# A two-layer decoder trunk on one core: three transposes moved from TensorE to VectorE in 32x32 blocks, x's sums of squares moved to GpSimd

## The chip, the core and the metric

The kernel runs on one core of a Trainium2 chip. A core has five engines that run their own instruction streams and meet through semaphores: TensorE (PE; its weight loads stand apart as PEld), VectorE (DVE), ScalarE (ACT), GpSimd (POOL) and SyncE (SP), which here issues nearly all transfers to the core's 16 DMA engines. Each engine takes its instructions in the order in which the program has them. The metric is the device time of one execution in microseconds, as the median of several runs; lower is better.

## What is computed

Batch 1, 256 positions, width 2048, two layers in float32. Layer 0 is a spatial gate (gMLP) beside cross-attention into 256 memory tokens, layer 1 latent attention (MLA) beside the same cross-attention; each is followed by a gated ConvFFN, and a last norm follows. Cut to what the change touches:

```python
def rmsnorm(x, g):
    return x * lax.rsqrt(jnp.mean(x * x, axis=-1, keepdims=True) + EPS) * g

def spatial_gating(z_u, z_v, g_v, w_sp, b_sp):
    u = gelu(z_u)
    v = rmsnorm(gelu(z_v), g_v)
    w = w_sp * jnp.tril(jnp.ones((CHUNK, CHUNK)))          # 12 heads of 128x128
    sv = einsum('gts,bnsgc->bntgc', w, v_in_chunks) + b_sp
    return u * sv

for l in range(2):
    z = rmsnorm(x, g_mix[l]) @ w_in[l]
    main = spatial_gating(...) if l == 0 else mla_attention(...)
    x = x + concat([main, memory_attention(...)]) @ w_out[l]
    x = x + conv_ffn(rmsnorm(x, g_ffn[l]), ...)
return rmsnorm(x, g_final)
```

## The kernel before

**Layout.** The residual `self.x` is kept in SBUF transposed: 16 blocks of 128 channels on the partitions, 256 positions along the free axis. The input `x` and the memory tokens come from HBM with the positions on the partitions (`xtok`, `mtok`), so they have to be turned. `token_transpose` (L395) does it on PE: four 128x128 transposes by the identity into one PSUM bank, from which `put_x` (L452) or `put_mem` (L446) writes the operand.

**Products.** Every weight chunk (128x1024, 512 KB) is loaded into `raw` (4 buffers), ACT writes a rounded high part `whi` (4 buffers) and DVE the rest `wlo` (5 buffers), with a gain factor where one applies (`chunk`, L98; L118 and L119 with gains and in two halves, L113 and L114 without). The activations are split the same way (`xhl`, `memhl`: high and low halves side by side). A product is the sum of three: high by high, high by low, low by high. `gemm_fm` (L158) holds the weights still and streams 256 positions: 16 matmuls with `whi` (L152, L153), then 8 with `wlo` (L155) for a chunk; `gemm_tm` (L190) streams 512 weight columns: 12 matmuls a chunk (L184, L185 with `wlo`, L186). Small pieces of other work are hung between chunks as hooks, by chunk number.

**The start.** `start` (L430) builds the memory keys and values of both layers, in this order: keys of layer 0 (`first_keys`, L477, its order written by hand), values of layer 0 (`gemm_tm`, 8 chunks, called c0 to c7 here), keys of layer 1 (`gemm_fm`, 8 chunks, called k0 to k7), values of layer 1. In the hooks of the last three the input x is loaded (four transfers of 512 KB), turned (8 calls for two blocks each: four transposes, two L245 on ACT and two L246 on DVE for `xhl` with the gain `g_mix`, and an ACT copy into `self.x`, L455), and its sums of squares are made by ACT from `xtok` (`token_squares`, L406, eight pieces) and reduced by DVE (`token_rstd`, L414). `spread` (L420) turns a per-position factor into a broadcast along the free axis: two diagonal matrices by DVE and two fp32 products. `scale_keys` (L466) multiplies the keys of layer 0 on POOL.

**Spatial weights.** `spatial_load` (L754) brings the 12 heads in one transfer, into the buffer that `memhl` held. `spatial_turn` (L760) transposes four at a time on PE, and DVE multiplies by the causal mask `keep` on the way out of PSUM (L765).

**The end.** In the second ConvFFN x is turned back into `xt` (positions on the partitions) by `turn` (L1110) in the hooks of one gemm: 32 transposes on PE, 8 ACT copies.

**Order.** The Tile scheduler sets the order on every engine by its own simulated timeline, but for the stretches under `manual_schedule`; the hooks only say where in the program a piece stands. In the stretch from c0 to k7 the hand-written order holds for SP alone, and only up to c7.

## Time and profile before

| | us |
|---|---|
| median of 3 runs (2058.31 to 2058.63) | 2058.41 |
| the profiled execution | 2058.79 |
| its span, first to last instruction | 2057.0 |
| PE busy | 2046.9 |
| DVE busy | 1396.0 |
| ACT busy | 1085.6 |
| POOL busy | 142.0 |
| transfers on SP's queue, mean share of the 16 DMA engines | 58.5% of the span |

The busy times are sums over stages with different limits, so only PE's says something by itself: hardly any time is left in which it has nothing to do. A matmul's busy time overlaps the next one's (a 128x256 matmul is shown with some 0.28 us, and the next starts 0.11 us later), so what a matmul costs is read from the distance of starts.

### The profile page before, as it was taken

To read this page: it belongs to the slowest core of one execution; us is meant where nothing else is said; L and a number is where in the kernel's file an instruction comes from. 1 tells how busy PE (TensorE), PEld (TensorE's weight loads), DVE (VectorE), ACT (ScalarE), POOL (GpSimd) and SP (SyncE) were. 2 spreads that over 40 slices of the span, in tenths; PEclk is the share of its full clock that TensorE was granted. 3 is DMA by queue.
4 is the path that set the end of the run, shared out by engine and by line. 5 is a ranking of instruction groups with operands and counts; after the bars stand their busy time and mean duration, and the time that the engine had idled before them with its cause. 6 is when DMAs were issued, how large, how long until landed. Compare 5 with 4: busy or idle time off the path is not lost.

```text
span 2057.0 us, 39914 instructions
## 1 busy us (share of the span) xinstructions
PE 2046.9 (100%) x16348; PEld 1979.9 (96%) x16348; DVE 1396.0 (68%) x2113; ACT 1085.6 (53%) x1588; POOL 142.0 (7%) x200
## 2 busy tenths in 40 slices
PE   9999999999999999999999999999999999999998
PEld 8989999999999999999999999999988999889996
DVE  6656766777656766457788786776765667646765
ACT  7754744555434555345555575455544555435554
POOL 0000013100000000000043241300000000000000
PEclk9999999999999999999999999999999999999999
DMA  8565555566556665566655635565655666556654
GB/s 288 188 217 176 160 193 198 190 195 195 195 195 195 193 193 193 194 193 194 195 195 176 187 118 178 187 204 177 193 193 194 196 195 195 187 193 195 197 181 154
DMA packets 207692, 392.58 MB, mean 191 GB/s; under 512 B 14158, under 2 KB 23188, under 8 KB 207380
## 3 DMA queue, kind: packets, MB, share of 16 engines
q1 hardware_dynamic: 207316, 389.48, 58.5%
q8 instruction: 128, 2.10, 0.4%
q10 hardware_dynamic: 192, 0.54, 0.1%
q14 instruction: 56, 0.46, 0.1%
HBM read 387.88 MB, written 2.10 MB: 190 GB/s over the span
## 4 chain that ended last, share of the span: by engine, by line
PE 99%; ACT 0%; DVE 0%; DMA 0%; issue 0%; ACTq 0%
PE ps L152 26%; PE ps L153 26%; PE ps L155 26%; PE ps L185 6%; PE ps L184 6%; PE ps L186 6%; PE ps L507 1%; PE ps L400 0%; PE ps L583 0%; PE ps L584 0%; PE ps L582 0%; PE ps L1001 0%; PE ps L790 0%; PE ps L1115 0%; PE ps L1029 0%; DMA graw<-in_g_mem 0%
## 5 line engine op out<-in xcount | busy, mean ns | idle before, releaser
L114 DVE TENSOR_TENSOR wlo<-raw,whi 128x1024 fp32r<-128x1024 f32 x660 | 818.4, 1243 | 531.1 <-ACT whi L113 525.0
L113 ACT ACTIVATE whi<-raw 128x1024 fp32r<-128x1024 f32 x660 | 700.6, 1062 | 857.8 <-PE ps L153 632.3
L152 PE MATMUL ps<-xhl,whi 128*128 128x256 f32 x3264 | 763.2, 277 | 0.0
L153 PE MATMUL ps<-xhl,whi 128*128 128x256 f32 x3264 | 761.2, 276 | 0.0
L153 PEld LDWEIGHTS ps<-xhl,whi 128*128 128x128 f32 x3264 | 612.9, 188 | 0.3
L152 PEld LDWEIGHTS ps<-xhl,whi 128*128 128x128 f32 x3264 | 612.7, 188 | 0.3
L155 PE MATMUL ps<-xhl,wlo 128*128 128x256 f32 x3264 | 436.7, 276 | 0.0
L155 PEld LDWEIGHTS ps<-xhl,wlo 128*128 128x128 f32 x3264 | 400.5, 188 | 0.0
L152 PE MATMUL ps<-h,whi 128*128 128x256 f32 x704 | 163.6, 276 | 0.0
L153 PE MATMUL ps<-h,whi 128*128 128x256 f32 x704 | 163.6, 276 | 0.0
L185 PE MATMUL ps<-wlo,h 128*128 128x512 f32 x354 | 137.2, 388 | 0.0
L184 PE MATMUL ps<-whi,h 128*128 128x512 f32 x354 | 136.8, 388 | 0.0
L186 PE MATMUL ps<-whi,h 128*128 128x512 f32 x354 | 136.8, 388 | 0.0
L153 PEld LDWEIGHTS ps<-h,whi 128*128 128x128 f32 x704 | 132.0, 188 | 0.0
L152 PEld LDWEIGHTS ps<-h,whi 128*128 128x128 f32 x704 | 131.8, 188 | 0.0
L152 PE MATMUL ps<-mainhl,whi 128*128 128x256 f32 x512 | 119.6, 277 | 0.0
L153 PE MATMUL ps<-mainhl,whi 128*128 128x256 f32 x512 | 119.3, 276 | 0.0
L694 ACT ACTIVATE c<-a,cT 128x256 f32<-128x256 f32 x176 | 99.4, 588 | 0.0
L153 PEld LDWEIGHTS ps<-mainhl,whi 128*128 128x128 f32 x512 | 96.0, 188 | 0.0
L152 PEld LDWEIGHTS ps<-mainhl,whi 128*128 128x128 f32 x512 | 95.9, 188 | 0.0
L155 PE MATMUL ps<-h,wlo 128*128 128x256 f32 x704 | 94.1, 276 | 0.0
L232 DVE TENSOR_TENSOR a<-ps,rbc 128x256 f32<-128x256 f32 x176 | 70.0, 418 | 27.6 <-PE ps L155 27.6
(321 smaller groups left out, 2258.6 us busy)
## 6 DMA issues: line engine op xcount, KB each, us to landing
raw<-in_w_ffn_up SPq DMA_DIRECT2D x352, 512.0 KB, 3.5
raw<-in_w_ffn_down SPq DMA_DIRECT2D x176, 512.0 KB, 3.9
raw<-in_w_out SPq DMA_DIRECT2D x64, 512.0 KB, 4.2
raw<-in_w_in_a SPq DMA_DIRECT2D x56, 512.0 KB, 4.3
raw<-in_w_mem_kv SPq DMA_DIRECT2D x31, 512.0 KB, 4.9
raw<-in_w_in_b SPq DMA_DIRECT2D x16, 512.0 KB, 4.6
raw<-in_w_kv_a SPq DMA_DIRECT2D x9, 512.0 KB, 3.6
raw<-in_w_uq SPq DMA_DIRECT2D x12, 384.0 KB, 3.8
```

What stands on the lines that cost most here:

```text
L113: nc.scalar.activation(hi[:, :n], raw[:, :n], AF.Copy)
L114: nc.vector.tensor_tensor(lo[:, :n], raw[:, :n], hi[:, :n].bitcast(F32), ALU.subtract)
L152: mm(acc[:, :S], wh, x[:, :S], start=first, stop=False)
L153: mm(acc[:, :S], wh, x[:, S:], start=False, stop=False)
L155: mm(acc[:, :S], wl, x[:, :S], start=False, stop=last)
L184: mm(acc, xh, wh, start=first, stop=False)
L185: mm(acc, xh, wl, start=False, stop=False)
L186: mm(acc, xl, wh, start=False, stop=last)
L232: self.nc.vector.tensor_tensor(out, acc[:, :S], r, ALU.mult)
L507: nc.tensor.matmul(acc[:, :S], w[:, o : o + P], x, start=k == 0 and n == 0, stop=k == NB - 1 and n == 2)
L694: nc.scalar.activation(c, a, AF.Identity, scale=w(2), bias=w(3))
```

## The change

- **x.** `block_load` replaces `token_load` for x: eight transfers of 256 KB with pieces of 32 elements (128 bytes) place x's 32x32 blocks in `xraw`, 32 channels of position blocks to a partition, two transfers for each of four calls. DVE's transpose of 32x32 blocks (`nc.vector.transpose`, 128x256 for one channel block) then writes `self.x`; `split_gain` reads it from SBUF instead of PSUM, and POOL squares and adds (`square_add`, 31 instructions). `x_rstd` makes the broadcast factor `rb` and the per-position factor `rt` from these sums, with one 128x256 product and two of one column. The 32 PE transposes of x, the eight ACT squares, the eight ACT copies and `spread(self.rb, self.rt)` go.
- **Hooks.** The loads of x start two chunks later; the turns stand in other hooks; `scale_keys` stands earlier. `diag` gets a second buffer.
- **Spatial weights.** Four transfers with 128-byte pieces instead of one with 512-byte rows; three DVE transposes 128x512; POOL multiplies by `keep` in place. 12 PE transposes and three DVE multiplications go.
- **The end.** Four DVE transposes 128x1024 into `xs` (2 buffers) and 16 transfers SBUF to SBUF with 128-byte pieces into `xt`, instead of 32 PE transposes and eight ACT copies.

```diff
@@ -392,6 +392,13 @@
         c = slice(k0 * P, k1 * P)
         self.nc.sync.dma_start(out=tok[:, :, c], in_=src.rearrange("(a p) c -> p a c", p=P)[:, :, c])
 
+    def block_load(self, src, raw, q, half):
+        s = src.rearrange("(i m) (k q j) -> q i m k j", m=8, q=4, j=32)
+        m = slice(4 * half, 4 * half + 4)
+        for p in (q, q + 1):
+            o = raw[32 * p : 32 * (p + 1), m].rearrange("i m k j -> i (m k) j")
+            self.nc.sync.dma_start(out=o, in_=s[p, :, m].rearrange("i m k j -> i (m k) j"))
+
     def token_transpose(self, tok, k0, k1, put):
         for k in range(k0, k1, 2):
             acc = self.psum()
@@ -421,7 +428,7 @@
         nc = self.nc
         acc = self.psum()
         for tb in range(2):
-            dg = self.tmp(self.cp, [P, P], "diag", 1)
+            dg = self.tmp(self.cp, [P, P], "diag", 2)
             nc.vector.tensor_scalar(dg, self.ident, r[:, tb : tb + 1], None, ALU.mult)
             nc.tensor.matmul(acc[:, tb * P : (tb + 1) * P], self.ones, dg, start=True, stop=True)
         nc.scalar.activation(out, acc[:, :S], AF.Copy)
@@ -436,10 +443,11 @@
         self.mv = [pool.tile([P, 2, MW], F32, name=self.uid("mv")) for pool in (self.mk, self.cp)]
         self.rt = self.cp.tile([P, 2], F32, name="rt0")
         self.rb = self.tmp(self.cp, [P, S], "rbc", 2)
+        self.ssum = self.tmp(self.cp, [P, S], "ssum", 2)
         with tc.tile_pool(name="st", bufs=1) as st:
             self.gp = st
             mtok = st.tile([P, 2, D], F32, name="mtok")
-            xtok = st.tile([P, 2, D], F32, name="xtok")
+            xraw = st.tile([P, 8, NB, 32], F32, name="xraw")
             mrt = st.tile([P, 2], F32, name="mrt")
             mrb = st.tile([P, S], F32, name="mrb")
 
@@ -449,19 +457,25 @@
                 nc.scalar.activation(hi, a, AF.Copy)
                 nc.vector.tensor_tensor(mhl[:, k : k + 2, S:], a, hi.bitcast(F32), ALU.subtract)
 
-            def put_x(k, acc):
-                for i in range(2):
-                    self.split_gain(self.xhl[k + i], acc[:, i * S : (i + 1) * S], self.gain("g_mix", k + i))
-                nc.scalar.activation(self.x[:, k : k + 2, :], acc.rearrange("p (k s) -> p k s", k=2), AF.Copy)
+            def xturn(k0, k1):
+                for k in range(k0, k1):
+                    nc.vector.transpose(out=self.x[:, k, :].rearrange("p (i m) -> p m i", m=8), in_=xraw[:, :, k, :])
+                    self.split_gain(self.xhl[k], self.x[:, k, :], self.gain("g_mix", k))
+                    self.square_add(self.ssum, self.x[:, k, :], k == 0, self.cp)
+
+            def x_rstd():
+                self.rstd_bc(self.rb, self.ssum, D)
+                acc = self.psum()
+                for tb in range(2):
+                    nc.tensor.matmul(acc[:, tb : tb + 1], self.ssum[:, tb * P : (tb + 1) * P], self.ones[:, :1], start=True, stop=True)
+                self.rstd(self.rt, acc[:, :2], D, self.cp, "rt")
 
             mload = lambda k0, k1: lambda: self.token_load(t["mem"][0], mtok, k0, k1)
             mturn = lambda k0, k1: lambda: self.token_transpose(mtok, k0, k1, put_mem)
-            xload = lambda k0, k1: lambda: self.token_load(t["x"][0], xtok, k0, k1)
-            xturn = lambda k0, k1: lambda: self.token_transpose(xtok, k0, k1, put_x)
+            xload = lambda n: lambda: self.block_load(t["x"][0], xraw, n % 2 * 2, n // 2)
+            xt = lambda k0, k1: lambda: xturn(k0, k1)
             mpart = st.tile([P, 2, 4], F32, name="mpart")
-            xpart = st.tile([P, 2, 4], F32, name="xpart")
             msq = lambda j: lambda: self.token_squares(mtok, mpart, j, st)
-            xsq = lambda j: lambda: self.token_squares(xtok, xpart, j, st)
 
             def scale_keys():
                 self.spread(mrb, mrt)
@@ -543,14 +557,14 @@
             hooks = [
                 None,
                 {
-                    0: [lambda: self.gains(("g_mix", "g_ffn", "g_kv")), xload(0, 4), msq(0), msq(1)], 1: [xload(4, 8), msq(2), msq(3)],
-                    2: [lambda: self.token_rstd(mpart, st, mrt), xload(8, 12)], 3: [xload(12, 16), xturn(0, 4)], 4: [self.masks],
-                    6: [lambda: self.gains(("g_v", "g_kv_lat", "g_q_lat"))],
+                    0: [lambda: self.gains(("g_mix", "g_ffn", "g_kv")), msq(0), msq(1)], 1: [msq(2), msq(3)],
+                    2: [lambda: self.token_rstd(mpart, st, mrt), xload(0)], 3: [xload(1)], 4: [self.masks, xload(2)], 5: [xload(3)],
+                    6: [lambda: self.gains(("g_v", "g_kv_lat", "g_q_lat"))], 7: [scale_keys],
                 },
-                {0: [xturn(4, 8)], 1: [scale_keys], 2: [xturn(8, 12)], 4: [xturn(12, 16)], 6: [xsq(0)]},
+                {3: [xt(0, 2)], 4: [xt(2, 4)], 5: [xt(4, 6)], 6: [xt(6, 8)], 7: [xt(8, 10)]},
                 {
-                    0: [xsq(1)], 1: [xsq(2)], 2: [xsq(3), lambda: self.conv_consts(0)], 3: [lambda: self.token_rstd(xpart, st, self.rt)],
-                    5: [lambda: self.spread(self.rb, self.rt), lambda: self.conv_consts(1)],
+                    0: [xt(10, 12)], 1: [xt(12, 14)], 2: [lambda: self.conv_consts(0)], 3: [xt(14, 16)],
+                    5: [lambda: self.conv_consts(1)], 7: [x_rstd],
                 },
             ]
             for l in range(2):
@@ -755,14 +769,16 @@
                 nc.sync.dma_start(out=bb, in_=t["b_sp"][0].rearrange("(o g) t -> o g t", o=1).to_broadcast([P, GH, P]))
                 raw = self.ap.tile([P, NB * 512], F32, tag="big", name=self.uid("wsp"))
                 spatial["raw"] = raw[:, :GW].rearrange("p (g s) -> p g s", g=GH)
-                nc.sync.dma_start(out=spatial["raw"], in_=t["w_sp"][0].rearrange("g t s -> t g s"))
+                blocks = t["w_sp"][0].rearrange("g (m i) (q j) -> q i g m j", i=32, j=32)
+                for q in range(4):
+                    o = raw[32 * q : 32 * (q + 1), :GW].rearrange("i (b j) -> i b j", j=32)
+                    nc.sync.dma_start(out=o, in_=blocks[q].rearrange("i g m j -> i (g m) j"))
 
             def spatial_turn(g):
-                acc = self.psum()
-                for i in range(4):
-                    nc.tensor.transpose(acc[:, i * P : (i + 1) * P], spatial["raw"][:, g + i, :], self.ident)
+                w4 = wT[:, g : g + 4, :]
                 k3 = self.keep.rearrange("p (g s) -> p g s", g=1).to_broadcast([P, 4, P])
-                nc.vector.tensor_tensor(wT[:, g : g + 4, :], acc.rearrange("p (g s) -> p g s", g=4), k3, ALU.mult)
+                nc.vector.transpose(out=w4, in_=spatial["raw"][:, g : g + 4, :])
+                nc.gpsimd.tensor_tensor(w4, w4, k3, ALU.mult)
 
             turns = {2 + i: [lambda i=i: spatial_turn(4 * i)] for i in range(3)}
             zhooks = ({2: [lambda: self.rope_angles(la)], 5: [spatial_load]}, {4: [self.rope_tables]}, turns)
@@ -1107,14 +1123,12 @@
             v = fin.tile([P, 2], F32, name="fv")
             nc.sync.dma_start(out=gb, in_=t["g_final"].rearrange("(o d) -> o d", o=1).to_broadcast([P, D]))
 
-            def turn(j):
-                acc = self.psum()
-                for tb in range(2):
-                    for i in range(2):
-                        o = (2 * tb + i) * P
-                        nc.tensor.transpose(acc[:, o : o + P], self.x[:, j + i, tb * P : (tb + 1) * P], self.ident)
-                nc.scalar.activation(xt[:, :, j * P : (j + 2) * P], acc.rearrange("p (a c) -> p a c", a=2), AF.Copy)
-
+            def turn(r):
+                xs = self.tmp(fin, [P, 2, NB, 32], "xs", 2)
+                nc.vector.transpose(out=xs, in_=self.x.rearrange("p k (a r j) -> p a k r j", a=2, j=32)[:, :, :, r, :])
+                o = xt[32 * r : 32 * (r + 1)].rearrange("j a (k q i) -> j q (a k) i", q=4, i=32)
+                for q in range(4):
+                    nc.sync.dma_start(out=o[:, q], in_=xs[32 * q : 32 * (q + 1)].rearrange("j a k i -> j (a k) i"))
 
             def tokens(j, tb, acc, last, half=None):
@@ -1162,8 +1176,7 @@
                     nc.sync.dma_start(out=self.out[0, rows, :1024], in_=y[:, :1024])
                     (nc.scalar if tb else nc.sync).dma_start(out=self.out[0, rows, 1024:], in_=y[:, 1024:])
 
-            turns = {4: [lambda: turn(0), lambda: turn(2)], 5: [lambda: turn(4), lambda: turn(6)],
-                     6: [lambda: turn(8), lambda: turn(10)], 7: [lambda: turn(12), lambda: turn(14)]}
+            turns = {2 * r: [lambda r=r: turn(r)] for r in range(4)}
             self.ffn(1, to_tokens=turns, tokens=tokens)
 
 
```

What the scheduler makes of it on SP, in the values of layer 0. `raw` is a weight chunk, `xtok` and `xraw` the two forms of x; each row is one transfer, or two where x2 stands. Before:

```order
L103 DMA raw_514<-in_w_mem_kv 128x2x512
L393 DMA xtok<-in_x 128x2x512
L103 DMA raw_546<-in_w_mem_kv 128x2x512
L393 DMA xtok<-in_x 128x2x512
L103 DMA raw_587<-in_w_mem_kv 128x2x512
L103 DMA raw_615<-in_w_mem_kv 128x2x512
L103 DMA raw_635<-in_w_mem_kv 128x2x512
```

Now:

```order
L103 DMA raw_512<-in_w_mem_kv 128x2x512
L400 DMA xraw<-in_x 32x64x32 x2
L103 DMA raw_545<-in_w_mem_kv 128x2x512
L400 DMA xraw<-in_x 32x64x32 x2
L103 DMA raw_567<-in_w_mem_kv 128x2x512
L400 DMA xraw<-in_x 32x64x32 x2
L103 DMA raw_597<-in_w_mem_kv 128x2x512
L400 DMA xraw<-in_x 32x64x32 x2
L103 DMA raw_619<-in_w_mem_kv 128x2x512
```

The chunks shown are c2 to c6 before (raw_514, 546, 587, 615, 635) and now (raw_512, 545, 567, 597, 619). Two of x's four loads stood ahead of c2's; now all four stand behind it, the last ahead of c6's.

DVE in the same stretch, from the `wlo` of c5 on. Now (`xhl_80` and `xhl_81` are the halves of x's operand; wlo_599 is c5, wlo_621 c6, wlo_648 c7, wlo_687 k0, wlo_719 k1):

```order
L119 SCALAR_TENSOR_TENSOR wlo_599<-raw_597,gT,whi_598 128x512 x2
L462 STREAM_TRANSPOSE xT<-xraw 128x8x32 x15
L246 SCALAR_TENSOR_TENSOR xhl_80<-xT,gT,xhl_80 128x256
L462 STREAM_TRANSPOSE xT<-xraw 128x8x32
L246 SCALAR_TENSOR_TENSOR xhl_80<-xT,gT,xhl_80 128x256 x2
L119 SCALAR_TENSOR_TENSOR wlo_621<-raw_619,gT,whi_620 128x512
L326 COPY gT<-ps_643 128x20
L119 SCALAR_TENSOR_TENSOR wlo_621<-raw_619,gT,whi_620 128x512
L246 SCALAR_TENSOR_TENSOR xhl_80<-xT,gT,xhl_80 128x256 x5
L119 SCALAR_TENSOR_TENSOR wlo_648<-raw_646,gT,whi_647 128x512 x2
L246 SCALAR_TENSOR_TENSOR xhl_81<-xT,gT,xhl_81 128x256 x4
L119 SCALAR_TENSOR_TENSOR wlo_687<-raw_685,gT,whi_686 128x512 x2
```

Before, the same chunks (wlo_617 is c5, wlo_637 c6, wlo_664 c7):

```order
L119 SCALAR_TENSOR_TENSOR wlo_589<-raw_587,gT,whi_588 128x512 x2
L246 SCALAR_TENSOR_TENSOR xhl_80<-ps_567,gT,xhl_80 128x256
L246 SCALAR_TENSOR_TENSOR xhl_80<-ps_577,gT,xhl_80 128x256
L119 SCALAR_TENSOR_TENSOR wlo_617<-raw_615,gT,whi_616 128x512
L416 TENSOR_REDUCE sums_534<-mpart 128x2
L255 TENSOR_SCALAR rtv_536<-sums_534 128x2
L119 SCALAR_TENSOR_TENSOR wlo_617<-raw_615,gT,whi_616 128x512
L119 SCALAR_TENSOR_TENSOR wlo_637<-raw_635,gT,whi_636 128x512
L326 COPY gT<-ps_659 128x20
L119 SCALAR_TENSOR_TENSOR wlo_637<-raw_635,gT,whi_636 128x512
```

All 16 turns of x, which were spread over c3 to k5, now stand between c5 and c6 in one block, and the 16 low halves of x follow among c6 to k2; nothing of a weight chunk stands between the first 15 transposes.

PE in the same stretch, from the last product of c6 on. Now:

```order
L185 MATMUL ps_448<-wlo_621,memhl_82 128x512
L186 MATMUL ps_448<-whi_620,memhl_82 128x512
L184 MATMUL ps_447<-whi_647,memhl_82 128x512
L184 MATMUL ps_448<-whi_647,memhl_82 128x512
L152 MATMUL ps_681<-memhl_82,whi_686 128x256
L153 MATMUL ps_681<-memhl_82,whi_686 128x256
L152 MATMUL ps_682<-memhl_82,whi_686 128x256
```

Two products of c7 with `whi` are followed by the 16 products of k0 with `whi` (the first three are shown), then by those of c7 that need `wlo`, and by those of k0 that need it. Before, all of c7 came ahead of k0.

## The prediction, made before the changed kernel ran

> **What bounds the kernel now.** First the page's head, engine shares and the chain that ended last, then the waits of PE over the whole span.
>
> ```profile
> span 2057.0 us, 39914 instructions
> PE 2046.9 (100%) x16348; PEld 1979.9 (96%) x16348; DVE 1396.0 (68%) x2113; ACT 1085.6 (53%) x1588; POOL 142.0 (7%) x200
> PE 99%; ACT 0%; DVE 0%; DMA 0%; issue 0%; ACTq 0%
> PE ps L474 <- DVE ones L283: 1.1, 1, 1.1
> PE ps L583 <- DVE pT L241: 0.4, 1, 0.4
> PE ps L325 <- DMA graw<-in_g_mem: 0.4, 1, 0.4
> ```
>
> The chain is PE for 99%, and PE's waits are three of 1.1 us or less. So a PE instruction that goes is time gained in full, wherever it stood, and every microsecond in which PE waits for something new is lost in full. All other engines have slack on average; what counts is whether one of them, for some 20 us, has more to do than PE leaves it time for. The stretch to look at is the one in which x is turned.
>
> **What goes from PE.** The timeline of PE, and two groups by line.
>
> ```profile
> 58.65 1.04 PE L400 MATMUL ps<-ident,xtok 128*128 128x128 f32 x8
> L763 PE MATMUL ps<-ident,wsp x12: 270/272/273, 156.6 to 163.4; 128*128 128x128 f32 x12
> L1115 PE MATMUL ps<-ident,xT x32: 271/272/273, 1405.8 to 1417.4; 128*128 128x128 f32 x32
> 61.35 1.07 PE L155 MATMUL ps<-memhl,wlo 128*128 128x256 f32 x8
> 62.27 0.38 PE L426 MATMUL ps<-diag,ones 128*128 128x128 f32 x2
> ```
>
> Eight transposes take 1.04 us from the first start to the last end; one lasts 0.272, so their starts lie (1.04 - 0.272)/7 = 0.11 us apart. That is what each costs PE. 32 + 12 + 32 = 76 go: 76 x 0.109 = **-8.3 us**. The eight matmuls of 256 columns lie as far apart, (1.07 - 0.28)/7 = 0.113, and the two halves of a `spread` product 0.38 - 0.27 = 0.11; `spread(rb, rt)` has four such instructions (0.45 us). Instead come a 128x256 fp32 product (two instructions of at most 0.22) and two of one column (two short ones each, at most 0.11): at most 0.88. I take **+0.3 us** for the difference. What ACT is spared (16 copies, eight squares) lies off the path.
>
> **x is turned on DVE: when it can start.** The timeline of ACT and DVE in the values of layer 0.
>
> ```profile
> 35.29 1.17 ACT L236 ACTIVATE kT<-ps 128x256 f32<-128x256 f32 x4
> 36.34 1.34 ACT L118 ACTIVATE whi<-raw,gT 128x512 fp32r<-128x512 f32 x2
> 37.57 0.64 ACT L409 ACTIVATE junk<-mtok 128x512 f32<-128x512 f32 x1
> 45.28 1.28 ACT L256 ACT_TABLE_LOAD   x1
> 57.44 2.74 DVE L119 SCALAR_TENSOR_TENSOR wlo<-raw,gT,whi 128x512 fp32r<-128x512 f32 x4 [1.83 <-ACT whi L118]
> ```
>
> In the new order ACT does, after the key copies (over at 36.3; some 0.3 earlier with the transposes ahead of them gone): c3's `whi` (1.23), three squares (0.61 each), c4's `whi`, a square, the table load (1.28) and the root (0.2): it ends at 36.05 + 1.23 + 1.83 + 1.23 + 0.8 + 1.28 + 0.2 = 42.6. DVE waits for that root, makes the memory factor and the diagonals (six short instructions, about 1.2 us), and c5's `wlo` (two of 0.67, from 2.74/4): it comes to the transposes at about 45.2.
>
> They need all of x. The windows of DMA, SP's timeline, and the one transfer with pieces under 512 bytes that there is before, `w_kv_a`'s last 64 columns (2048 pieces of 256 bytes).
>
> ```profile
> 28.00:30.00 2.00, 2.00 (x20) 2.00 (x20) 1.94 (x3) 2.00 (x5) 0.00 (x0) 1.00 1.03 390
> 34.00:36.00 2.00, 2.00 (x11) 1.63 (x10) 1.40 (x3) 2.00 (x8) 0.00 (x0) 1.00 1.03 374
> 38.00:40.00 2.00, 2.00 (x10) 1.62 (x10) 0.96 (x2) 2.00 (x6) 0.00 (x0) 1.00 0.79 285
> 31.44 4.35 SPq L103 DMA_DIRECT2D raw<-in_w_mem_kv  x3
> 1104.89 0.37 SPq L128 DMA_DIRECT2D raw<-in_w_kv_a  x1
> 1107.00:1108.00 1.00, 1.00 (x12) 1.00 (x11) 0.18 (x2) 0.84 (x2) 0.00 (x0) 1.00 1.28 275
> ```
>
> The last two columns of a window are the DMA share and GB/s. From 28 to 36 the 16 engines are full, so transfers queue there. A chunk of 512 KB takes 1.34 us (0.524 MB at 390). Pieces of 256 bytes went at 275 GB/s, 0.93 ns each: a piece of 128 bytes lies between half of that, 0.47 (if bytes decide), and 0.93 (if the piece does); I take 0.7, in the middle, as no row favours an end. One call for x (two transfers, 4096 pieces) is then 2.9 us (1.9 to 3.8). Ahead of the last one in the queue from 28 on: c3, c4, c5 (4.0), the rest of c2 (0.4) and the other three, with its own 11.6: 28 + 16 = 44, and some 2 us to landing: x is there at **46** (42 to 49.5). DVE waits 0.8 us for it. [...]
>
> **What DVE has to do then, and what POOL does to it.** No row shows a 32x32 transpose. The nearest are DVE's operations on 256 elements, and how these run when POOL computes.
>
> ```profile
> 1304.16 1.42 DVE L643 TENSOR_TENSOR xT<-ps,xT 128x256 f32<-128x256 f32 x4 [0.63 <-PE ps L155]
> 1306.86 3.35 DVE L246 SCALAR_TENSOR_TENSOR xhl<-xT,gT,xhl 128x256 fp32r<-128x256 f32 x4
> 60.10 0.87 DVE L246 SCALAR_TENSOR_TENSOR xhl<-ps,gT,xhl 128x256 fp32r<-128x256 f32 x2
> 1305.81 2.60 POOL L275 TENSOR_TENSOR ssum<-ssum,sq 128x256 f32<-128x256 f32 x2
> 1308.38 1.55 POOL L274 TENSOR_TENSOR sq<-xT 128x256 f32<-128x256 f32 x2
> L119 DVE SCALAR_TENSOR_TENSOR wlo<-raw,gT,whi 128x512 fp32r<-128x512 f32 x4 | 3.9, 992 | 0.5 <-ACT whi L118 0.5
> L119 DVE SCALAR_TENSOR_TENSOR wlo<-raw,gT,whi 128x512 fp32r<-128x512 f32 x96 | 72.7, 793 | 20.6 <-ACT whi L118 20.4
> 1100.30 2.17 POOL L274 TENSOR_TENSOR sq<-ck 128x256 f32<-128x256 f32 x2
> ```
>
> This is what decides, so the rows one by one. In `w_out` DVE makes x's low halves from SBUF (third stage of the same helper, L246) while POOL squares: four take 3.35 us, 0.84 each. From PSUM, without POOL, two take 0.87: 0.40 each once the overlap of 0.07 is taken off. L643, which reads PSUM, is not slowed (1.42/4 = 0.35) though POOL is at work. So two SBUF inputs beside POOL cost 0.44 more each. L119 reads two SBUF inputs too: its four in the window 1100 to 1104, beside POOL's squares, have a mean of 992 ns, against 0.75 alone: 0.25 more. The change puts 31 POOL operations (two squares and two sums took 1.55 + 2.60, so about 30 us in all) and the four of `scale_keys` into the very stretch in which all of x's low halves, now from SBUF, and the `wlo` stand on DVE. POOL has its input as soon as the first transpose is done, so it is busy from 46 to about 80.
>
> The transposes: 0.40 each as for 256 elements from SBUF. Below, 0.33 (256 elements of the 0.35 above); above, 0.84 if POOL holds them up as it does L246. They have one input, and the row of slow ones has two, so I take the lower side.
>
> From c5's `wlo` to k1's: 16 transposes (6.4), 15 low halves of x at 0.84 (12.6), eight halves of `wlo` at 0.67 + 0.25 (7.4), a small copy (0.1): 26.5. k1's `wlo` is there at 46 + 26.5 = **72.5**.
>
> PE came to k1's products with `wlo` at 61.35 before. 16 transposes ahead of it go (-1.74), the spread of the memory factor now comes ahead of it (+0.45): 60.1. Since PE works through the rest without a gap, what it has waited by then is 72.5 - 60.1 = **12.4 us**; about 4 of it at c6, ahead of which the block stands, the rest at c7, k0 and k1. The products of k0 that the new order puts ahead of c7's `wlo` only shift it between these. At k2 DVE needs 0.84 + 1.84 and PE 0.9 + 1.8: it gets no worse, and from k3 on no low halves of x are left and a chunk's 1.3 to 1.8 is less than PE's 2.72.
>
> **Moved edits with no price, and their cover.** Spatial weights and the end, from the timelines.
>
> ```profile
> 104.23 0.69 ACT L567 ACTIVATE mv<-ps,mrt 128x512 f32<-128x512 f32 x1 [0.65 <-PE ps L186]
> 113.51 1.23 DVE L114 TENSOR_TENSOR wlo<-raw,whi 128x1024 fp32r<-128x1024 f32 x1 [1.50 <-ACT whi L113]
> 1331.89 4.57 DVE L114 TENSOR_TENSOR wlo<-raw,whi 128x1024 fp32r<-128x1024 f32 x3
> 1337.67 1.23 DVE L114 TENSOR_TENSOR wlo<-raw,whi 128x1024 fp32r<-128x1024 f32 x1 [1.21 <-ACT whi L113]
> ```
>
> The first mixer product starts when the memory values end, at 104.2. DVE writes the `wlo` of its chunk 6 at 113.5, and PE needs it after six chunks of 2.72, at 120.5. In front of it now come the rest of the rstd of x (4 us, of which 1.5 fit the gap shown) and three transposes of 128x512 (0.7 each, 512 elements at L119's pace), which also wait for the four transfers (6144 pieces, 4.3 us, beside 2 us of `b_sp`, from 106: 113 to 114). That makes `wlo` 117 to 118: cover of 2 to 3 us, and cost nothing; if the pieces were twice as slow, 2 us. At the end four transposes of 128x1024 (1.23 each, as L114) stand where DVE is full until 1336.5 and idle after; the third and fourth wait for a buffer, so for four transfers of 0.7 us behind up to four chunks on SP's queue. There `wlo` is four chunks, 10 us, ahead of PE, and DVE loses 5 us and the waits. If a transfer took 8 us to come back, PE would wait. I take 0. SP's own queue: two x transfers (0.45 us of issue each) between chunks, which wait for their buffers anyway.
>
> **The sum.** Against the profiled execution, 2058.79 (span 2057.0): -8.3 + 0.3 + 12.4 = +4.4, so 2063.2. The median of the runs is 0.4 lower: **2063 us**.
>
> **Rivals.**
> - *DVE keeps pace, the transposes are simply gained.* For it: DVE is idle for 20.6 us before L119 in all, and POOL may be held up rather than DVE. Then 15 low halves at 0.40 and eight `wlo` halves at 0.67 give 46 + 17.9 = 63.9, a wait of 3.8: 2054. With x at 43 and no wait at all, 2050.4. It decides for the other side as soon as the mean collision costs DVE under 0.2 us instead of 0.25 to 0.44. Against it: the 32 L246 rows from SBUF have a mean of 895.
> - *The transposes are slow or x is late.* 0.84 each adds 7.0; x at 49.5 adds 3.5; both, 2073. [...]
> - *PE's clock falls.* PE ended its last matmul at 2048.9, and the granted clock (third from the end) shows this:
>
> ```profile
> 2048.00:2050.00 2.00, 0.90 (x8) 0.69 (x6) 1.50 (x5) 0.51 (x2) 0.00 (x0) 1.00 1.02 410
> 2052.00:2054.00 2.00, 0.00 (x0) 0.00 (x0) 0.41 (x1) 0.60 (x1) 0.00 (x0) 0.54 0.60 242
> ```
>
>   half speed some 3 us after PE stopped. A wait of 4 us at c6 could bring that about. While DVE sets the pace PE's 10.4 us of work up to k1 would take 20.8, in the 19 that DVE needs: +2; and as long again to recover: +4, 2067. [...]
>
> **How the numbers follow.** A measurement of this kernel tells 0.2%, 4.1 us, from no change. My forecast (DVE behind by 8.5 to 16 us, so 2058.5 to 2066.5): 50%, of which 28 above 2062.5 and 22 below. Slow transposes or late x: 20%, slower. The clock: 8%, slower. DVE nearly keeps pace (2052.5 to 2057): 15%, of which 10 faster. No wait at all: 7%, faster. So faster 0.17, same 0.27, slower 0.56. The range leaves out the gain without any wait and the worst of late x: 2052.5 to 2073; the likeliest case's own is 2058.5 to 2066.5.
>
> **What would show it.** Right: PE waits for `wlo` (L119) from about 49 to 73, 12 us in all, and nowhere else for long; L246 at 0.84 or more there; transposes at 0.33 to 0.42; 76 matmuls less elsewhere with no new wait; x landed about when DVE comes to it. Wrong: L246 and L119 at their short times beside POOL, PE waits on DMA, waits at 115 to 125 or 1330 to 1350, or transposes much longer than 256 elements.

## The result, and the profile after

The changed kernel takes 2072.97 us (median of 6 runs, 2072.33 to 2074.21), the kernel before, run on the same chips, 2058.52: a ratio of 1.007, 95% interval 1.0057 to 1.0082. It is slower by 14.5 us, 10 us beyond the predicted time; it lies inside the widest range of the prediction, 2052.5 to 2073, by 0.03 us only, and three of the six runs lie above it. The profiled execution took 2072.33 and its span is 2070.6, 13.6 above that of before. First the head of its page, engine shares and chain:

```profile
span 2070.6 us, 39828 instructions
PE 2047.4 (99%) x16274; PEld 1975.9 (95%) x16274; DVE 1418.3 (68%) x2135; ACT 1074.7 (52%) x1557; POOL 171.2 (8%) x234
PE 96%; DVE 2%; SPq 1%; ACT 0%; DMA 0%; issue 0%; DVEq 0%; ACTq 0%
```

The span less PE's busy time is 23.2 us, and was 10.1: PE is idle 13.1 us more. Its busy time is 0.5 more, although 76 transposes are gone, which should have made it 8.0 less. So PE's time has two losses: 13.1 in waits, and 8.5 in work that was slower. The chain, 99% PE before, now runs for 3% through DVE and SP's queue. The waits of PE (total, times, longest):

```profile
PE ps L185 <- DVE wlo L119: 6.4, 1, 6.4
PE ps L155 <- DVE wlo L119: 2.4, 3, 1.7
PE ps L184 <- ACT whi L118: 2.2, 1, 2.2
PE ps L325 <- DMA graw<-in_g_q_lat: 1.8, 1, 1.8
```

All four are new, 12.8 us together, and lie between 43 and 85 us, in the values of layer 0 and the keys of layer 1: one for c6's `wlo` (L185), three for those of k0 and k2 (L155), one for c4's `whi`, one for a gain row. DVE's timeline shows what it did there:

```profile
45.10 1.42 DVE L119 SCALAR_TENSOR_TENSOR wlo<-raw,gT,whi 128x512 fp32r<-128x512 f32 x2 [4.37 <-ACT whi L118]
50.08 1.41 DVE L119 SCALAR_TENSOR_TENSOR wlo<-raw,gT,whi 128x512 fp32r<-128x512 f32 x2 [0.90 <-ACT whi L118]
53.49 7.19 DVE L462 STREAM_TRANSPOSE xT<-xraw 128x256 f32<-128x256 f32 x15 [1.99 <-DMA xraw<-in_x]
64.87 4.08 DVE L246 SCALAR_TENSOR_TENSOR xhl<-xT,gT,xhl 128x256 fp32r<-128x256 f32 x5
68.88 2.37 DVE L119 SCALAR_TENSOR_TENSOR wlo<-raw,gT,whi 128x512 fp32r<-128x512 f32 x2
78.97 2.24 DVE L119 SCALAR_TENSOR_TENSOR wlo<-raw,gT,whi 128x512 fp32r<-128x512 f32 x2
```

c4's `wlo` at 45.1, c5's at 50.1, then 15 transposes that waited 2 us for x, then low halves of x with a chunk's `wlo` among them; the last row is k1's. From 53.5 to 84.3 DVE has no gap. The chain in order of time leads back from there to x's last load (start, duration), and SP's timeline shows the loads as they were issued:

```profile
45.58 7.73 DMA xraw<-in_x
```

```profile
26.44 4.54 SPq L400 DMA_DIRECT2D xraw<-in_x  x2
31.07 1.21 SPq L103 DMA_DIRECT2D raw<-in_w_mem_kv  x1
32.32 5.29 SPq L400 DMA_DIRECT2D xraw<-in_x  x2
...
39.25 4.12 SPq L400 DMA_DIRECT2D xraw<-in_x  x2
...
45.07 3.74 SPq L400 DMA_DIRECT2D xraw<-in_x  x2
```

Two of x's transfers keep SP's queue for 3.7 to 5.3 us, and a chunk's load can be issued only behind them. The last of x lands at 45.58 + 7.73 = 53.3. The chunks come late with them: c3's, c4's and c5's `whi` start 5 to 6 us apart, where PE needs 2.72 for a chunk (12 products, whose starts lay 0.227 apart before the change). That is the 2.2 us for c4's `whi`, for whose chunk ACT had to wait:

```profile
44.35 1.34 ACT L118 ACTIVATE whi<-raw,gT 128x512 fp32r<-128x512 f32 x2 [2.62 <-DMA raw<-in_w_mem_kv]
```

The work that was slower is seen in windows of half a microsecond, whose third column from the end is the granted TensorE clock (the first number after the window is its length, the second PE's busy time). These six are those in which the clock changes; between the first and second, third and fourth, and fifth and sixth it is 0.50, elsewhere 1.00:

```profile
46.00:46.50 0.50, 0.50 (x2) 0.40 (x3) 0.50 (x2) 0.48 (x3) 0.00 (x0) 0.62 0.46 117
49.50:50.00 0.50, 0.50 (x3) 0.12 (x1) 0.00 (x0) 0.50 (x2) 0.00 (x0) 0.96 1.12 132
56.00:56.50 0.50, 0.37 (x3) 0.23 (x2) 0.50 (x2) 0.50 (x2) 0.50 (x1) 0.86 0.77 250
70.00:70.50 0.50, 0.50 (x5) 0.50 (x5) 0.50 (x2) 0.43 (x1) 0.50 (x1) 0.98 0.00 0
76.50:77.00 0.50, 0.40 (x2) 0.40 (x3) 0.50 (x2) 0.37 (x1) 0.50 (x1) 0.84 0.00 0
80.00:80.50 0.50, 0.50 (x5) 0.50 (x5) 0.50 (x2) 0.38 (x1) 0.50 (x1) 0.74 0.00 0
```

A mean of 0.62 in the first is 0.12 us at full and 0.38 at half clock, so it fell at 46.12. Read in this way it is at half from 46.12 to 49.54, from 56.36 to 70.02 and from 76.84 to 80.26. Summed over all windows from 30 to 110, PE's busy time times the missing part of the clock is 7.0 us; before, the same sum is 0. That is most of the 8.5. The other 1.5 is not assigned.

How PE's time divides into waits and slow work does not yet say what set the end. That is read from the chain in order of time:

```profile
53.49 3.53 DVE xT L462 x8
...
82.09 2.18 DVE wlo L119 x2
84.31 1.06 PE ps L155 x7
```

From 32 to 84.31 us the chain holds no instruction of PE: it goes through SP's queue, x's last load and DVE, until PE can go on with k2's `wlo`, for which it waited 0.4 us. All half clock is over at 80.26. So up to 84.31 the slow clock only took the place of waiting: at full clock PE would have come earlier to the same `wlo` and stood there longer.

### The profile page after: what moved, and what is told of

Its sections match the earlier page's. It is cut to its first block, busy times and chain, and to the rows that moved or that the text cites. A ratio compares the mean times of both kernels' runs of the same rounds, so it can differ in the third digit from the quotient of the medians.

```text
span 2070.6 us, 39828 instructions
## 1 busy us (share of the span) xinstructions
PE 2047.4 (99%) x16274; PEld 1975.9 (95%) x16274; DVE 1418.3 (68%) x2135; ACT 1074.7 (52%) x1557; POOL 171.2 (8%) x234
## 4 chain that ended last, share of the span: by engine, by line
PE 96%; DVE 2%; SPq 1%; ACT 0%; DMA 0%; issue 0%; DVEq 0%; ACTq 0%
PE ps L152 25%; PE ps L153 25%; PE ps L155 25%; PE ps L184 6%; PE ps L186 6%; PE ps L185 6%; PE ps L521 1%; DVE xhl L246 1%; SPq L400 0%; DVE wlo L119 0%; DMA xraw<-in_x 0%; DVE xT L462 0%; PE ps L597 0%; PE ps L598 0%; PE ps L596 0%; PE ps L1017 0%
## 5 line engine op out<-in xcount | busy, mean ns | idle before, releaser
L155 PE MATMUL ps<-xhl,wlo 128*128 128x256 f32 x3264 | 436.5, 276 | 0.0
L155 PEld LDWEIGHTS ps<-xhl,wlo 128*128 128x128 f32 x3264 | 400.4, 188 | 0.0
L185 PE MATMUL ps<-wlo,h 128*128 128x512 f32 x354 | 137.2, 388 | 0.0
L118 ACT ACTIVATE whi<-raw,gT 128x512 fp32r<-128x512 f32 x96 | 64.0, 716 | 62.0 <-PE ps L153 21.5
L155 PE MATMUL ps<-h,wlo 128*128 128x256 f32 x704 | 94.1, 276 | 0.0
```

The lines of the kernel that those rows point to most:

```text
L118: nc.scalar.activation(hi[:, s], raw[:, s], AF.Copy, scale=gains[k])
L155: mm(acc[:, :S], wl, x[:, :S], start=False, stop=last)
L185: mm(acc, xh, wl, start=False, stop=False)
```

## The experiments

Twelve kernels, five questions. In the tables "idle" is the span less PE's busy time, "clock" the sum just described (from 30 to 110 or 130 us), both of the profiled execution.

### Which part of the change costs

`x_only` has the change's part on x, with spatial weights and end as before. `no_x` is the opposite. `x_only`, against the changed kernel:

```diff
-                for q in range(4):
-                    o = raw[32 * q : 32 * (q + 1), :GW].rearrange("i (b j) -> i b j", j=32)
-                    nc.sync.dma_start(out=o, in_=blocks[q].rearrange("i g m j -> i (g m) j"))
+                nc.sync.dma_start(out=spatial["raw"], in_=t["w_sp"][0].rearrange("g t s -> t g s"))
...
-            turns = {2 * r: [lambda r=r: turn(r)] for r in range(4)}
+            turns = {4: [lambda: turn(0), lambda: turn(2)], 5: [lambda: turn(4), lambda: turn(6)],
+                     6: [lambda: turn(8), lambda: turn(10)], 7: [lambda: turn(12), lambda: turn(14)]}
```

`no_x`, against the kernel before:

```diff
+                for q in range(4):
+                    o = raw[32 * q : 32 * (q + 1), :GW].rearrange("i (b j) -> i b j", j=32)
+                    nc.sync.dma_start(out=o, in_=blocks[q].rearrange("i g m j -> i (g m) j"))
...
+                nc.vector.transpose(out=w4, in_=spatial["raw"][:, g : g + 4, :])
+                nc.gpsimd.tensor_tensor(w4, w4, k3, ALU.mult)
...
+            turns = {2 * r: [lambda r=r: turn(r)] for r in range(4)}
```

> Only x's part of the change; the spatial weights and the end (residual to token order) are as before. Theory (the loss is all in x's part, and the two other parts give their transposes' time, 44 x 0.109 = 4.8 us, without a new wait): 2073.0 + 4.8 = 2077.8. Rival (the late loads of the spatial weights or the transfers of the residual cost something that the trace does not show as a wait): 2073 or below.

> The complement: x is loaded and turned as before, the spatial weights and the end as in the change. Theory: 2058.5 - 4.8 = 2053.7. Rival (128-byte pieces hold up the weights, or DVE's waits for a free buffer at the end reach PE): 2056 or more.

| kernel | median us (runs) | ratio, interval | span | PE busy | idle | clock |
|---|---|---|---|---|---|---|
| before | 2058.52 (6) | | 2057.0 | 2046.9 | 10.1 | 0 |
| changed | 2072.97 (6) | 1.007, 1.0057 to 1.0082 | 2070.6 | 2047.4 | 23.2 | 7.0 |
| `x_only` | 2077.39 (4) | 1.0092, 1.0076 to 1.0107 | 2075.8 | 2051.3 | 24.5 | 5.1 |
| `no_x` | 2054.51 (10) | 0.998, 0.997 to 0.9989 | 2052.8 | 2042.2 | 10.6 | 0 |

Both as expected. x's part costs 18.9, the other two parts gain 4.0, and the sum, +14.9, is the whole change's +14.5. PE's longest waits in `no_x` are two of before and one of half a microsecond:

```profile
PE ps L474 <- DVE ones L283: 1.1, 1, 1.1
PE ps L325 <- DMA graw<-in_g_mem: 0.5, 1, 0.5
PE ps L152 <- ACT whi L113: 0.5, 1, 0.5
```

44 transposes at 0.109 are 4.8; the spans differ by 4.2. So at the spatial weights and at the end DVE's transposes and their transfers do lie beside other work.

### What POOL's squares cost

`no_squares` leaves 30 of POOL's 31 squares and sums out; the order of everything else is the same.

```diff
-                    self.square_add(self.ssum, self.x[:, k, :], k == 0, self.cp)
+                    if k == 0:
+                        self.square_add(self.ssum, self.x[:, k, :], True, self.cp)
```

> The change, but POOL forms the square of x's first block of features only; the 15 other squares and their sums are left out, so the sum of squares is not x's. Every other engine's order is the same. Theory (POOL beside DVE makes x's low halves 0.85 instead of 0.40 us and the low halves of the weights 1.15 instead of 0.67, some 11 us from 61 to 84): low halves at 0.40 to 0.45 and 0.67 to 0.75, DVE no longer behind after the first of them; the wait at 57 to 64 gets 1.5 shorter at most, since the transposes stand ahead of it. 5 us less: 2067.7 (2066 to 2069.5). Rival (DVE is late because of x and the transposes alone): 2072 to 2073.

Measured: 2067.74 (4 runs), ratio 1.0043 (1.0027 to 1.006), 5.2 us below the changed kernel. DVE's timeline, the rows that answer to those at 64.87 and 68.88 above:

```profile
66.53 2.06 DVE L246 SCALAR_TENSOR_TENSOR xhl<-xT,gT,xhl 128x256 fp32r<-128x256 f32 x5
68.51 1.40 DVE L119 SCALAR_TENSOR_TENSOR wlo<-raw,gT,whi 128x512 fp32r<-128x512 f32 x2
```

Five low halves in 2.06 instead of 4.08, two `wlo` halves in 1.40 instead of 2.37: beside POOL a low half costs 0.4 more and a `wlo` half 0.5. Both read two tensors from SBUF. The transposes, with their one input, are spared: 15 of them take 7.19 us with POOL at work, and 7.26 in `no_squares`, where POOL has one instruction beside them. What it is that DVE and POOL contend for, no run shows.

But the long wait stays:

```profile
PE ps L185 <- DVE wlo L119: 7.3, 1, 7.3
```

It is over before the squares matter: c6's `wlo` stands behind the transposes and only three low halves. What the squares cost comes after it: without them DVE is done with k1's `wlo` at 75.3 instead of 81.2, and PE does not wait for a `wlo` of k0 to k2 any more. The kernel's idle time is 22.8 (23.2 with the squares), its clock sum 3.9 (7.0), its span 2067.2. That is 3.4 less than the changed kernel's, not 5.2, because this profiled execution, the slowest of the four, lost 1.7 to half clock from 8.8 to 12.2 us, before any of this; the medians are the better measure.

### Whether it is the pieces, or the block of transposes

`long_pieces` loads x in rows of 8 KB, `pinned` leaves the loads alone and holds each transpose at its place in the program, so that DVE does not take them ahead of the chunk that they stand behind.

```diff
-        s = src.rearrange("(i m) (k q j) -> q i m k j", m=8, q=4, j=32)
+        s = src.rearrange("(p i h) c -> p i h c", i=32, h=2)
...
-            o = raw[32 * p : 32 * (p + 1), m].rearrange("i m k j -> i (m k) j")
-            self.nc.sync.dma_start(out=o, in_=s[p, :, m].rearrange("i m k j -> i (m k) j"))
+            o = raw[32 * p : 32 * (p + 1), m].rearrange("i m k j -> i (m k j)")
+            self.nc.sync.dma_start(out=o, in_=s[p, :, half])
```

```diff
-                    nc.vector.transpose(out=self.x[:, k, :].rearrange("p (i m) -> p m i", m=8), in_=xraw[:, :, k, :])
+                    i = nc.vector.transpose(out=self.x[:, k, :].rearrange("p (i m) -> p m i", m=8), in_=xraw[:, :, k, :])
+                    tc.keep_in_program_order(i)
```

> The change, but x is loaded in rows of 8 KB (the same bytes to the same tile through the same eight transfers, so what lies in the tile is not what the transposes need); the scheduler, which knows the length of a transfer, puts the transposes between the low halves of the fifth and sixth chunk. Theory (the pieces of 128 bytes make x land at 53 instead of 42 and hold up the weights' chunks): x lands at 41 to 44, no wait for the fifth chunk, the first transpose 9 to 11 us earlier and with it the end of DVE's work: 2063.5 (2061 to 2066). Rival (not the pieces but DVE's work beside POOL sets the time): 2070 to 2073.

> The change, but each transpose of x is held in DVE's order behind the low halves of the chunk that it is written after (pairs after k3 to k7 and the first chunks of the next stage) instead of all 16 ahead of c6. Loads and POOL's squares as in the change. Theory (what x's late transfers cost before c6, 5.8 us, stays; the wait at c6 goes; then a chunk's two halves, two transposes and two low halves of x beside POOL take DVE 4.6 us against PE's 2.72 for eight chunks, 15 less the 5 to 6 that DVE is ahead): 2068 (2064 to 2072). Rival (only the place of the block was wrong): 2061 or less.

`long_pieces` missed by far: 2081.45 (4 runs), ratio 1.0113 (1.0098 to 1.0128). PE's waits:

```profile
PE ps L433 <- DVE diag L432: 12.7, 1, 12.7
PE ps L325 <- DMA graw<-in_g_v: 5.2, 1, 5.2
```

With x's loads shorter on SP the order around them moved: the memory's root, and with it the diagonals (L432), now came behind 16 transposes, and a gain row late. So the kernel does not tell what it was made for. Nor did the rows of 8 KB bring x much earlier: its transposes began at 49.5 instead of 53.5. It shows that the block of transposes costs what happens to stand behind it.

`pinned` is 2063.63 (10 runs, 2061.06 to 2064.78), ratio 1.0022 (1.0012 to 1.0031): 9.3 below the changed kernel by one edit that changes neither work nor transfers. It lies between the two expectations, just below the first one's range. The waits that stay:

```profile
PE ps L184 <- ACT whi L118: 3.5, 3, 2.7
PE ps L185 <- DVE wlo L119: 2.7, 3, 1.6
```

The larger part is now for `whi`, which needs the chunk, so for chunks' loads behind x's; the rest is still for DVE. One stretch of half clock is left, 1.7 us in the sum.

### What makes x's transfers slow

From `pinned`, three kernels change one or both of the ways in which x's transfers differ from a chunk's: pieces of 128 bytes, and 32 partitions each. `pinned_wide` is `pinned` with each transfer on 128 partitions (all other instructions in the same order), `pinned_mid` is `pinned` with pieces of 2048 bytes, `pinned_wide_long` has both. The three edits, in the order `pinned_mid`, `pinned_wide`, `pinned_wide_long`:

```diff
-        s = src.rearrange("(i m) (k q j) -> q i m k j", m=8, q=4, j=32)
+        s = src.rearrange("(m i) (q c) -> q i m c", i=32, q=4)
...
-            o = raw[32 * p : 32 * (p + 1), m].rearrange("i m k j -> i (m k) j")
-            self.nc.sync.dma_start(out=o, in_=s[p, :, m].rearrange("i m k j -> i (m k) j"))
+            o = raw[32 * p : 32 * (p + 1), m].rearrange("i m k j -> i m (k j)")
+            self.nc.sync.dma_start(out=o, in_=s[p, :, m])
```

```diff
-        s = src.rearrange("(i m) (k q j) -> q i m k j", m=8, q=4, j=32)
-        m = slice(4 * half, 4 * half + 4)
+        s = src.rearrange("(p a) (k q j) -> a q p k j", a=2, q=4, j=32)
...
-            o = raw[32 * p : 32 * (p + 1), m].rearrange("i m k j -> i (m k) j")
-            self.nc.sync.dma_start(out=o, in_=s[p, :, m].rearrange("i m k j -> i (m k) j"))
+            self.nc.sync.dma_start(out=raw[:, 4 * half + p], in_=s[half, p])
```

```diff
-        s = src.rearrange("(i m) (k q j) -> q i m k j", m=8, q=4, j=32)
-        m = slice(4 * half, 4 * half + 4)
+        s = src.rearrange("(p a) (q c) -> a q p c", a=2, q=4)
...
-            o = raw[32 * p : 32 * (p + 1), m].rearrange("i m k j -> i (m k) j")
-            self.nc.sync.dma_start(out=o, in_=s[p, :, m].rearrange("i m k j -> i (m k) j"))
+            self.nc.sync.dma_start(out=raw[:, 4 * half + p].rearrange("i k j -> i (k j)"), in_=s[half, p])
```

> The kernel before, and x's eight transfers bring pieces of 2048 bytes instead of 128 (the same bytes to the same tile; what lies in it is not what the transposes need). Theory (the short pieces hold up the weights' chunks and the rows of gains: 2.2 and 1.8 us of waits, and the clock): no wait for transfers before c6, 7 us less than the kernel before: 2061 (2058 to 2065). Rival (that x goes in eight transfers to 32 partitions each, not the pieces, is what delays): within 2 us of the kernel before.

> The kernel with held transposes (2063.6), and each of x's eight transfers brings its 2048 pieces of 128 bytes to all 128 partitions (16 pieces each) instead of 32 (64 pieces each); what lies in the tile is then not what the transposes need. Every engine's order is the same. Theory P (the number of pieces decides, wherever they go): c3 to c5 wait as before, 2063.6 within 1.5. Theory Q (that a transfer goes to 32 partitions decides, which would also explain why pieces of 2048 bytes to 32 partitions gained only 2 us): the waits before c6 are gone, 6 us less: 2057.5 (2056 to 2059).

> The fourth of a square: the kernel with held transposes, x's eight transfers in pieces of 2048 bytes to all 128 partitions (one piece each), at the change's places in SP's queue; every engine's order as in the kernel with pieces of 2048 bytes to 32 partitions. Theory (either the short pieces or the 32 partitions alone hold the transfers up, so that taking one away gained 0 to 2 us; with both gone the 16 engines move 370 to 390 GB/s again): no wait for a chunk before c6, 5 us less than that kernel: 2056.5 (2055 to 2058). Rival (x's place in the queue, two chunks later than before the change, is what delays the chunks behind it): 2060 or more.

| kernel | pieces, partitions | median us (runs) | ratio, interval | idle | clock |
|---|---|---|---|---|---|
| `pinned` | 128 B, 32 | 2063.63 (10) | 1.0022, 1.0012 to 1.0031 | 17.4 | 1.7 |
| `pinned_mid` | 2048 B, 32 | 2061.61 (10) | 1.002, 1.0007 to 1.0033 | 16.8 | 3.1 |
| `pinned_wide` | 128 B, 128 | 2063.21 (10) | 1.0021, 1.0012 to 1.003 | 18.3 | 0 |
| `pinned_wide_long` | 2048 B, 128 | 2056.09 (11) | 0.9986, 0.9978 to 0.9995 | 13.1 | 1.7 |

One window, 32 to 40 us, in which chunks and x are under way together, of before and of these four in the table's order (the last column is GB/s, the one ahead of it the share of the 16 DMA engines):

```profile
32.00:40.00 8.00, 8.00 (x45) 6.74 (x44) 4.74 (x8) 8.00 (x20) 0.00 (x0) 1.00 0.95 342
```

```profile
32.00:40.00 8.00, 8.00 (x41) 6.75 (x40) 4.03 (x7) 6.29 (x17) 0.00 (x0) 1.00 1.08 167
```

```profile
32.00:40.00 8.00, 8.00 (x42) 6.71 (x41) 3.07 (x6) 5.45 (x14) 0.00 (x0) 1.00 1.05 223
```

```profile
32.00:40.00 8.00, 8.00 (x41) 6.80 (x40) 4.30 (x7) 6.90 (x19) 0.00 (x0) 1.00 0.90 178
```

```profile
32.00:40.00 8.00, 8.00 (x40) 6.69 (x39) 5.27 (x8) 7.96 (x21) 0.00 (x0) 1.00 0.97 332
```

The engines are as full everywhere, and move half of it with 128-byte pieces, on 32 or on 128 partitions, two thirds with long pieces on 32, and what they moved before only with both. The time of `pinned_mid` is the one expected, but not for the reason expected: PE came to the 288th product with weights (before the change, the last one of layer 0's values) 6.7 us later than before, in `pinned` 6.4, so nothing had been freed there, and with 2.0 less than `pinned` the kernel fits its rival as well. The time of `pinned_wide` is the one of theory P, but in its profile PE is less late at that product (3.4), and loses more later. Only with both gone is PE ahead there, by 1.7, and only then do 7.5 us go in the whole. So either alone holds the transfers up; the place in the queue, which is the same in all four, is not the cause. What was measured of the two is the step from 223 to 332 GB/s, from 32 partitions to 128, and that from 178 to 332, from 128 bytes to 2048; why either slows the engines, no run shows.

### Whether the idea can be made to pay

x's result needs short pieces on 32 partitions, so the next kernels leave them as they are and spread them. `late_pool` issues one transfer of x per chunk from c6 to k5, and holds the transposes behind k7 and the values of layer 1.

```diff
-                {3: [xt(0, 2)], 4: [xt(2, 4)], 5: [xt(4, 6)], 6: [xt(6, 8)], 7: [xt(8, 10)]},
...
+                    0: [xload(2)], 1: [xload(3)], 2: [xload(4)], 3: [xload(5)], 4: [xload(6)], 5: [xload(7)],
+                    7: [xt(0, 2)],
...
+                    0: [xt(2, 4)], 1: [xt(4, 6)], 2: [xt(6, 8), lambda: self.conv_consts(0)], 3: [xt(8, 10)], 4: [xt(10, 12)],
+                    5: [xt(12, 14), lambda: self.conv_consts(1)], 6: [xt(14, 16)], 7: [x_rstd],
```

`late_act` is `late_pool` with ACT taking the squares from `xraw`, in eight instructions, and DVE putting the sums in place:

```diff
-                    self.square_add(self.ssum, self.x[:, k, :], k == 0, self.cp)
...
+                    tc.keep_in_program_order(nc.scalar.activation(junk, src, AF.Square, accum_out=xpart[:, m : m + 1]))
...
+                tc.keep_in_program_order(nc.vector.tensor_tensor(self.ssum.rearrange("p (i m) -> p i m", m=8), a, b, ALU.mult))
```

`best` mends `late_act` in three places: the turns begin a chunk earlier, and the loads and transposes of the spatial weights are held at their places in the program:

```diff
-                    7: [xt(0, 2)],
+                    6: [xt(0, 2)], 7: [xt(2, 4)],
...
-                    nc.sync.dma_start(out=o, in_=blocks[q].rearrange("i g m j -> i (g m) j"))
+                    tc.keep_in_program_order(nc.sync.dma_start(out=o, in_=blocks[q].rearrange("i g m j -> i (g m) j")))
...
-                nc.vector.transpose(out=w4, in_=spatial["raw"][:, g : g + 4, :])
+                tc.keep_in_program_order(nc.vector.transpose(out=w4, in_=spatial["raw"][:, g : g + 4, :]))
```

`best2` is `best` with the four transfers of the spatial weights behind one chunk each of the next stage:

```diff
-                for q in range(4):
-                    o = raw[32 * q : 32 * (q + 1), :GW].rearrange("i (b j) -> i b j", j=32)
-                    tc.keep_in_program_order(nc.sync.dma_start(out=o, in_=blocks[q].rearrange("i g m j -> i (g m) j")))
...
+            blockhooks = {q: [lambda q=q: spatial_block(q)] for q in range(4)}
```

> The change, with x's eight transfers spread, one behind each chunk from c6 to k5, and the transposes held behind k7 and the seven chunks after it, two each; squares on POOL as in the change. Theory (transfers fit between the chunks; DVE beside POOL is behind as in the first of these four, but nothing else is lost): 2059.5 (2055 to 2063), all of the wait for low halves in the eight chunks after k7. Rival (POOL costs nothing when DVE's work is spread): 2050.5.

> As the third, and the squares are formed by ACT from x as it lies after the load (a sum per token and partition group, eight operations of 512 elements), so that POOL does nothing there; one DVE product spreads them for the sum over partitions. Theory (76 transposes of PE for nothing, DVE at 3.2 us against 2.72 for eight chunks, within what it is ahead): 2058.5 - 8.3 + 0.3 = 2050.5 (2050 to 2053). Rival (pieces of 128 bytes hold up the weights wherever they are sent): PE waits for chunks in k0 to k7, 2054 or more.

> The kernel with x's loads spread and ACT's squares (2058.2), mended at three places that its trace shows: the transfers of the spatial weights are held on SP behind the rows of positions and the bias (PE waited 2.6 us for the positions, then ran 1.3 at half clock), the transposes of the spatial weights behind the chunk that they are written after, and the transposes of x begin one chunk earlier. Theory (only PE's 76 transposes are left of the change): 2050.5 (2049.5 to 2053). Rival (x's pieces or DVE's 3.2 us for a chunk cost PE time wherever they stand): 2055 or more.

> The kernel with spread loads, ACT's squares and the three mended places (2055.5), whose trace shows one chunk 8.9 us late behind the four transfers of the spatial weights and 3.1 us of PE time lost from 115 to 137. Here those four go one behind each chunk of the next stage. Theory: the 3.1 us come back, what stays lost is 1.6 at the values of layer 1 where DVE has 3.2 us for a chunk: 2052.4 (2051 to 2053.5). Rival (the loss from 115 to 137 is DVE's angles and not the transfers): 2055.

| kernel | median us (runs) | ratio, interval | span | idle | clock |
|---|---|---|---|---|---|
| `late_pool` | 2063.6 (9) | 1.0024, 1.0014 to 1.0034 | 2063.0 | 18.4 | 1.7 |
| `late_act` | 2058.23 (10) | 0.9995, 0.9986 to 1.0004 | 2054.5 | 13.7 | 1.7 |
| `best` | 2055.47 (11) | 0.9985, 0.9976 to 0.9994 | 2052.8 | 13.0 | 0 |
| `best2` | 2052.14 (6) | 0.9969, 0.9957 to 0.9981 | 2049.8 | 10.6 | 0 |

`late_pool` came out 4 us above what was expected: spread, the loads no longer hold the chunks up, but POOL's sum is what ends last:

```profile
PE ps L265 <- POOL ssum L275: 2.5, 1, 2.5
PE ps L152 <- ACT whi L113: 2.4, 1, 2.4
```

The first wait is the sum's. The second has nothing to do with x: it lies at 1367, in the second ConvFFN, where SP's queue is full of the end's transfers from `xs` to `xt` and a chunk comes late behind them; another 1.6 us of half clock follow it, outside the windows of the table.

`late_act` took the first wait away and gained 5.4, but missed its number by 8. PE stopped for the transpose of the positions, whose load stood on SP behind two transfers of the spatial weights, and ran at half clock from 114 to 117. In `best` that wait is gone, and the next one shows on SP and then on ACT:

```profile
PE ps L352 <- issue: 2.2, 1, 2.2
```

```profile
105.41 8.56 SPq L793 DMA_DIRECT2D wsp<-in_w_sp  x4
```

```profile
120.09 1.06 ACT L113 ACTIVATE whi<-raw 128x1024 fp32r<-128x1024 f32 x1 [8.85 <-DMA raw<-in_w_in_a]
```

The first row is a wait of PE in `late_act`, the others are of `best`: four transfers with short pieces keep SP for 8.6 us, and ACT waits 8.9 for the chunk of `w_in_a` behind them. It is x's pattern once more, and it put `best` on its rival's side. `best2` puts them one by one, and landed where it was expected. Its longest wait of PE was there before:

```profile
PE ps L503 <- DVE ones L283: 1.1, 1, 1.1
```

Its span is 7.2 below that of before, of the 8.0 that the transposes are worth. It is faster than both kernels; the intervals of `late_act`, `best` and `best2` each overlap the next one's, so the single steps are less sure than the way from 1.007 to 0.9969.

## Why the prediction came out as it did

Direction and mechanism were right: DVE gets more to do between c6 and k1 than PE leaves it time for, and what PE loses there is more than the transposes gave. The time was 10 us too low, and outside the likeliest case's own range. What happened is the second rival, x late, which had 20% and whose worst came to 2073; that the widest range just holds the result is luck.

- **The 76 transposes, -8.0: right.** `no_x` shows its part of it and `best2` nearly all.
- **Spatial weights and end at no cost: right** as the change has them, by `no_x`. The covers were thin all the same: the one at `w_in_a` gave way when `late_act` and `best` moved x's work towards it, the one at the end in `late_pool`.
- **POOL and the low halves, 0.84: right**, 0.82 in five; the `wlo` halves beside POOL were 0.92 by the forecast and 1.2 on the chip.
- **The transposes, 0.40: a little low.** (7.19 - 0.62)/14 = 0.47; over 16 this is 1.1 us. POOL doesn't slow them (7.19 for 15 beside it, 7.26 in `no_squares`), as was taken.
- **x is there at 46 (42 to 49.5): wrong, and the step that failed.** It was 53.3, later than the bound of 49.5. The step took 0.7 ns for a piece, its author's estimate from the one row of 256-byte pieces, let the transfers queue at that price and added 2 us to landing, for which it shows no row: a chunk of the ConvFFN lands 3.5 us after its issue before the change (`w_ffn_up`, median), x's eight transfers 5.8 to 7.9. The runs show that with short pieces or 32 partitions the full engines move 167 to 223 GB/s instead of some 340, chunks and x together, and SP's timeline that the chunks' issues are held up as well. This made c4's `wlo` late, so that DVE came to the transposes at 51.5 instead of 45.2, and it is the source of two waits that the forecast did not have (2.2 for `whi`, 1.8 for the gain row).
- **The wait, 12.4: mis-sized, though the waits came to 12.8.** DVE was done with k1's `wlo` at 81.2 instead of 72.5, 8.7 later. Of that 7.5 is the later start; of the rest, the transposes took 1.1 more, the `wlo` halves 1.3 more and the low halves of x 1.2 less than in the forecast. By the forecast's own step PE then loses 81.2 - 60.1 = 21.1 us up to k1. It spent 7.0 of them on slow work instead of waiting, so that the waits look like the forecast by accident.
- **The clock, 0 in the sum: no loss of its own, though it fell three times.** It was a rival with 8% and +4, for one fall at c6. PE lost 7.0 to it, but all before 80.26, and it still had to wait for DVE at 84.31. The rival's own working went this way: of 10.4 us lost to half clock while DVE sets the pace, it let only 2 stay. Leaving the clock out of the sum was not the error; it would have been one, had PE set the pace behind the falls.

The sum again, with DVE's measured end: -8.3 + 0.3 + 21.1 = 13.1, and the span is 13.6 longer; the 0.4 for which PE waited at k2 is most of what is left. That the clock took the place of waits is read from the chain of the changed kernel, and no run takes it away by itself. That x's short pieces on 32 partitions make its loads slow is shown by the four kernels with held transposes; for the changed kernel's own order it rests on its trace.

## What to carry to other kernels

Taking a microsecond off the engine that sets the end pays only if the engine that takes the work over has time in that very stretch. If it has not, ask when that engine is done, for that sets the loss; a slow clock between two waits for it added nothing here (7.0 us of PE's time), and is to be priced only behind the last of them. Transfers in pieces of 128 bytes or to 32 partitions brought what the full engines moved here from some 340 to 167 to 223 GB/s, and made the chunks behind them late: issue them one by one between the large ones, early enough that nobody needs them soon. And hold moved work at its place in the order, for a scheduler that sees 16 ready instructions may put them all ahead of the one that PE waits for; with these three, and the squares on ACT instead of POOL, the same idea went from 14.5 us lost to 6.8 gained.
